# A hybrid trunk layer in fp32: the retention state term as three rounded matmuls, masks loaded per head, three instead of four transposes for a head's last keys, and the last output rows in four pieces

## The chip, the cores and the metric

The kernel runs on one core of a Trainium2 chip. The metric is device time in microseconds (us) of one launch; lower is better. The engines are named as the profile names them: PE (matmul), PEld (weight loads of PE), DVE (vector), ACT (scalar), POOL (GpSimd) and SP (which here issues most of the DMAs). Each engine runs its own instructions in a fixed order and waits on semaphores for the others.

## The reference, cut to what matters

One layer over 1024 positions of width 1024, all in fp32: an RMS norm, one wide input projection, a retention branch and a recurrent branch side by side, a gated merge, an output projection, then a gated MLP and a last RMS norm. Nearly all of the arithmetic is in the large projections. The change touches the retention branch, which has four heads with keys of 128 and values of 256:

```python
    def step(state, inp):
        qi, ki, vi = inp
        scores = jnp.einsum("bhid,bhjd->bhij", qi, ki) * intra_decay
        out = (jnp.einsum("bhij,bhjv->bhiv", scores, vi)
               + jnp.einsum("bhid,bhdv->bhiv", qi * q_decay[:, :, None], state))
        state = (state * chunk_decay[:, None, None]
                 + jnp.einsum("bhjd,bhjv->bhdv", ki * k_decay[:, :, None], vi))
        return state, out
...
    y_a = (o * jax.nn.silu(g_ret.astype(jnp.float32))).astype(x.dtype) @ w_ret_o[l]
...
    return rms_norm(x, norm_f_w)
```

## The kernel before, in words

**Large products.** Every large projection is a set of 128x512 matmuls on operands that were split beforehand into a rounded high part and a rounded rest (`split`: an ACT copy that rounds, line 597, and a DVE subtraction, line 598). A product takes three such rounded passes, high by high, high by low and low by high (`PASSES`). The large matmuls are issued at line 848 (`mm_fast`), those of the values at 1606; the blocks of weights (`w` tiles) are split up to seven ahead of their use. Sums of blocks (lines 683 to 692, 871, 877) save one product in eight.

**Side work.** While PE works through a list of jobs, generators in the queue `back` are advanced a little after each product. Among them are the retention heads (`retention_head`, after `rotary_head`), the recurrent blocks (`lru_block`, matmuls at 1257), and sums of weights that are put away for later (`four_sums`, 1429 to 1441). A head works through its 1024 positions in eight blocks of 128, numbered `h` (half) and `b`. For each block PE makes the scores (1372), DVE masks them (1375), the result is split (597 and 598 on `sm` tiles), PE multiplies them by the values in three rounded passes (1380), and adds the term of the carried state: one matmul of the unrounded query block and the unrounded state `rst` (1382), 28 times in all, since a head's first block has no state. Then ACT copies the output (1387), PE makes the state's increment from keys and values in three passes (1392), DVE adds it to the decayed state (1396, or 1394 for the first), and DVE takes the statistics of the output (1400, 1401). The state has two buffers, `rst[0]` and `rst[1]`, which change places. `keys` turns a half's keys by four transposes (1332), scales them (1337) and splits them; the last block of a head makes no increment, yet its keys are transposed too.

**Constants.** The tile `cst` holds small columns, four 128x128 masks, one per head, and the identity. It is loaded in one DMA (1695); before that its first columns serve as a place for the first columns of `x` (1630 to 1635).

**The end.** The last rows leave in `final_half`: when the last product of 128x256 is done, ACT squares it (2059), DVE adds (2060), POOL takes the power (2066), and ACT and DVE each scale a 128x512 tile (2076, 2074), which then leaves by one DMA each (2077), after the two tiles of `final` (2087, 2090).

**Order.** The kernel is written in program order, and then a planner (`Plan`) reads its instructions with their dependencies, and writes an order for each engine by its own table of durations. It tries 150 drafts with random shifts and keeps one; the program is then built again with this order as a chain on each engine. A small edit therefore changes the order of unrelated instructions as well.

Of the kernel before, what the change touches and what calls it, by code (L numbers as in the profile page):

```python
# [38 lines left out]

C_INVF, C_KDEC, C_GEPS, C_MASK, C_ID = 0, 1, 5, 9, 9 + 512  # L40
NCONST = 9 + 512 + 128
# [512 lines left out]
def tile_trunk_layer(ctx, tc, x, xt, front, positions, params, consts, normf, w_in, w_v, w_ro, w_lo,  # L554
# [10 lines left out]
    U = Units(pool, "u", NU, [P, TH], now)  # L565
    sm = Units(pool, "sm", 6, [P, P], now)
    psg = Units(pps, "g", 6, [P, TH], now)
# [4 lines left out]
    par = pool.tile([P, NPAR], F32, tag="par", name="par")  # L572
    cst = pool.tile([P, NCONST], F32, tag="cst", name="cst")
    ident = cst[:, C_ID:C_ID + P]
# [487 lines left out]
    rcol = pool.tile([P, 8], F32, tag="rcol", name="rcol")  # L1062
    row = pool.tile([8, P], F32, tag="row", name="row")
    kdr = pool.tile([P, HEADS, 8], F32, tag="kdr", name="kdr")

    def x_rms():
# [20 lines left out]
        PE.transpose(j[0:8, 0:P], rcol, ident)  # L1087
        S.copy(row, j[0:8, 0:P])
        psa.put(j)
        SY.dma_start(r_d.rearrange("h (t p) -> (h t) p", p=P), row)  # L1090
        for h in range(2):
# [211 lines left out]
    qk, gg = {}, {}  # L1303
    rst = [pool.tile([P, 256], F32, tag=f"state{i}", name=f"state{i}") for i in range(2)]
    bst = pool.tile([P, 4, 6], F32, tag="bst", name="bst")
# [22 lines left out]
    def keys(hd, qk, h):  # L1328
        ps = psa.get()
        for b in range(4):  # L1330
            bs = slice(128 * b, 128 * b + 128)
            PE.transpose(ps[:, bs], qk[1, h][:, bs], ident)
        t = get()
        for b in range(4):
            bs = slice(128 * b, 128 * b + 128)
            n = 4 * h + b
            S.activation(t[:, bs], ps[:, bs], AF.Copy, scale=kdr[:, hd, n:n + 1])
        kd[h] = split(t)
        put(t, late=SOONER)
        psa.put(ps)  # L1340

    def v_tile(hd, h, g):
        t = get()
        SY.dma_start(t, v_d[hd, 2 * h + g].rearrange("p b c -> p (b c)"))
        return t

    def retention_head(hd, qk):
        cur = 0
        tick = now[0]
        raw = {(0, g): v_tile(hd, 0, g) for g in range(2)}  # L1350
        yield from landed(tick)

# [5 lines left out]
        v_split(0, 0)  # L1358
        mask = cst[:, C_MASK + 128 * hd:C_MASK + 128 * hd + 128]
        for h in range(2):  # L1360
            for b in range(4):
# [11 lines left out]
                s = sm.get()  # L1373
                n = 4 * h + b
                V.scalar_tensor_tensor(s, p1[:, 0:128], rcol[:, n:n + 1], mask, ALU.mult, ALU.mult)
                psa.put(p1)
# [4 lines left out]
                if not first:  # L1381
                    PE.matmul(p2[:, 0:256], qk[0, h][:, bs], rst[cur], start=False, stop=True)  # L1382
                sm.put(*s)
# [5 lines left out]
                if not last:  # L1389
                    p3 = psa.get()  # L1390
                    for n, (i, j) in enumerate(PASSES):
                        PE.matmul(p3[:, 0:256], kd[h][i][:, bs], v[j][:, vs], start=n == 0, stop=n == 2)  # L1392
                    if first:
                        V.tensor_copy(rst[1 - cur], p3[:, 0:256])
                    else:
                        V.scalar_tensor_tensor(rst[1 - cur], rst[cur], GAM128[hd], p3[:, 0:256],
                                               ALU.mult, ALU.add)
                    psa.put(p3)
                    cur = 1 - cur
                V.bn_stats(bst[:, b, :], o)  # L1400
# [161 lines left out]
    def values():  # L1562
# [23 lines left out]
        def x_set(nm, j, first=False):  # L1586
            hi, lo = get(F32R), get(F32R)
            b, w = xs[nm, j], cst[:, j:j + 1] if nm == "B11" else wn(nm, j)
            if not first:
                S.activation(hi, b, AF.Copy, scale=w)  # L1590
            for c in (slice(0, P), slice(P, TH)) if first else (slice(0, TH),):
                if first:
                    V.tensor_scalar(hi[:, c], b[:, c], w, None, ALU.mult)
                V.scalar_tensor_tensor(lo[:, c], b[:, c], w, hi.bitcast(F32)[:, c], ALU.mult, ALU.subtract)
            h1[nm, j] = (hi, lo)
# [35 lines left out]
        nc.scalar.dma_start(cst[:, 0:first], front[:, 0:first])  # L1631
        xs["B11", 0] = cst[:, 8:8 + TH]
        V.tensor_copy(par[:, 0:8], cst[:, 0:8])
        wload("A11", 0)
        SY.dma_start(cst[:, first:8 + TH], front[:, first:])
        wload("A11", 1)
# [36 lines left out]
        for j in range(4):  # L1673
            f[j], t[j], s[j] = get(), get(), vget()
            S.activation(f[j], xs["B11", j], AF.Copy, scale=wn("B11", j))
            if j:
                put(xs["B11", j])
            V.tensor_add(s[j], raw["A21", j], raw["A22", j])
# [14 lines left out]
        for j in range(4):  # L1693
            xload("B22", j)
        SY.dma_start(cst, consts)
        back.append(x_rms())
# [356 lines left out]
    def final_half(u, s):  # L2053
# [16 lines left out]
        put(j)  # L2070
        for c in range(2):
            t = fin.pop((0, 0)) if c == 0 else o
            if c:
                V.tensor_scalar(t, t, r, None, ALU.mult)
            else:
                S.activation(t, t, AF.Copy, scale=r)
            (SY if c else nc.scalar).dma_start(out[128 * 3:128 * 4, TH * c:TH * c + TH], t)
            put(t)

# [111 lines left out]
```

## Time and profile before

| What | Value |
|---|---|
| median of 3 runs | 1567.7 us (1567.51 to 1568.17) |
| the profiled execution's own time | 1566.78 us |
| its span, first to last instruction | 1565.0 us |
| PE busy | 1557.1 us, 99% of the span |
| DVE busy | 1343.9 us, 86% |
| ACT busy | 952.5 us, 61% |
| granted PE clock | 0.999 |
| moved by DMA | 278.97 MB, mean 178 GB/s |

The shares are means over stages: retention lies between about 230 and 433 us of the span, the merge and output projections between 640 and 890, the MLP behind that. Since PE is busy nearly always, what counts is where PE waits, what the other engines have to deliver to it in a stage, and what lies before its first and behind its last matmul. The profiled execution took 0.9 us less than the median of the runs.

### The profile page before, as it was taken

The numbers are of one execution on the slowest core, as the hardware profiler recorded it, in microseconds if no ns is written. First come the engines' busy times: TensorE is split into PE (matmuls) and PEld (weight loads), VectorE is DVE, ScalarE is ACT, GpSimd is POOL, SyncE is SP. The second block draws the span as 40 slices with busy tenths as digits, with TensorE's granted clock in tenths as the row PEclk, the third lists the DMA queues.
The fourth block names the chain that finished last, engine by engine and source line by source line (L and its number), as shares of the span: only waits on it lengthen the run. The fifth ranks groups of instructions, "written<-read, shape, count | busy, mean of one in ns | idle before, by whom it ended". The sixth has DMA issues, their size and how long they took to land.

```text
span 1565.0 us, 21570 instructions
## 1 busy us (share of the span) xinstructions
PE 1557.1 (99%) x7057; PEld 1290.7 (82%) x7057; DVE 1343.9 (86%) x2397; ACT 952.5 (61%) x1675; POOL 61.0 (4%) x81
## 2 busy tenths in 40 slices
PE   9999999999999999999999999999999999999998
PEld 7888888888888888888888888888888888888887
DVE  8999988998899988999998899777777778887875
ACT  8558766766568777855456665455454547554653
POOL 0001000000000000000000001000000000000000
PEclk9999999999999999999999999999999999999999
DMA  9344334454364346875995336444444476777752
GB/s 328 121 139 130 115 129 124 140 187 155 114 203 142 101 135 186 266 276 174 315 315 173 106 115 223 141 135 142 134 138 144 146 239 196 250 266 256 265 187 80
DMA packets 157713, 278.97 MB, mean 178 GB/s; under 512 B 17048, under 2 KB 29728, under 8 KB 157600
## 3 DMA queue, kind: packets, MB, share of 16 engines
q1 hardware_dynamic: 152080, 261.79, 51.3%
q0 software_dynamic: 4224, 13.64, 2.7%
q10 hardware_dynamic: 1296, 2.17, 0.4%
q8 instruction: 55, 0.90, 0.2%
q14 instruction: 58, 0.48, 0.1%
HBM read 192.59 MB, written 83.89 MB: 177 GB/s over the span
## 4 chain that ended last, share of the span: by engine, by line
PE 93%; DMA 3%; DVE 2%; ACT 1%; issue 1%; SPq 0%; POOLq 0%; POOL 0%; DVEq 0%; ACTq 0%
PE g L848 81%; PE g L1606 5%; PE a L1257 3%; DMA w<-mix_d 1%; PE a L1382 1%; PE a L1380 1%; DMA u<-tw_d 1%; PE a L1392 1%; DVE w L598 0%; PE a L1884 0%; PE a L1372 0%; PE a L1451 0%; DMA w<-w_lo 0%; DMA sg_d<-u 0%; DVE u L598 0%
## 5 line engine op out<-in xcount | busy, mean ns | idle before, releaser
L848 PE MATMUL g<-u,w 128*128 128x512 f32 x6060 | 1412.6, 391 | 0.0
L848 PEld LDWEIGHTS g<-u,w 128*128 128x128 f32 x6060 | 1129.7, 188 | 229.0
L597 ACT CAST w<-w 128x512 fp32r<-128x512 f32 x519 | 319.0, 621 | 334.4 <-PE g L848 240.3
L598 DVE TENSOR_TENSOR w<-w,w 128x512 fp32r<-128x512 f32 x519 | 352.9, 684 | 84.4 <-ACT w L597 81.0
L597 ACT CAST u<-u 128x512 fp32r<-128x512 f32 x253 | 151.2, 619 | 60.6 <-DVE u L1239 7.5
L598 DVE TENSOR_TENSOR u<-u,u 128x512 fp32r<-128x512 f32 x253 | 166.7, 682 | 4.3 <-ACT u L597 4.0
L900 ACT COPY u<-g 128x512 f32<-128x512 f32 x148 | 86.4, 583 | 61.3 <-PE g L848 58.4
L877 DVE TENSOR_TENSOR u<-g,u 128x512 f32<-128x512 f32 x146 | 100.1, 686 | 22.1 <-PE g L848 16.8
L1936 DVE SCALAR_TENSOR_TENSOR u<-u,par,u 128x511 f32<-128x511 f32 (+1 forms) x96 | 71.6, 746 | 12.8 <-ACT u L1933 12.2
L1606 PE MATMUL g<-w,u 128*128 128x512 f32 x252 | 58.7, 389 | 0.0
L1606 PEld LDWEIGHTS g<-w,u 128*128 128x128 f32 x252 | 47.2, 188 | 9.9
L1941 POOL DMA_DIRECT2D ff_d<-u x48 | 36.2, 754 | 444.6 <-DVE u L1940 434.2
L683 DVE TENSOR_TENSOR w<-w,w 128x512 f32<-128x512 f32 x72 | 49.2, 683 | 2.7 <-DMA w<-ff_d 1.4
L897 ACT COPY g<-g 128x512 f32<-128x512 f32 x70 | 40.4, 577 | 17.8 <-PE g L848 17.6
L1257 PE MATMUL a<-u,u 128*128 128x512 f32 x192 | 50.4, 390 | 0.5 <-ACT u L597 0.5
L686 DVE TENSOR_TENSOR w<-w,w 128x512 f32<-128x512 f32 x72 | 49.3, 684 | 0.7
L689 DVE TENSOR_TENSOR w<-w,w 128x512 f32<-128x512 f32 x72 | 49.2, 683 | 0.3 <-DMA w<-w_lo 0.2
L692 DVE TENSOR_TENSOR w<-w,w 128x512 f32<-128x512 f32 x72 | 49.2, 683 | 0.4
L1933 ACT ACTIVATE u<-u,par 128x512 f32<-128x512 f32 x48 | 39.1, 816 | 7.8 <-DVE u L877 7.0
L1257 PEld LDWEIGHTS a<-u,u 128*128 128x128 f32 x192 | 35.9, 188 | 8.6 <-ACT u L597 1.3
L871 DVE TENSOR_TENSOR u<-u,u 128x512 f32<-128x512 f32 x34 | 23.2, 687 | 20.5 <-ACT u L900 20.4
L1940 DVE TENSOR_TENSOR u<-u,u 128x512 f32<-128x512 f32 x48 | 32.9, 687 | 5.4 <-ACT u L1939 5.4
(216 smaller groups left out, 1158.8 us busy)
## 6 DMA issues: line engine op xcount, KB each, us to landing
w<-w_in SPq DMA_DIRECT2D x96, 256.0 KB, 2.8
w<-w_up SPq DMA_DIRECT2D x96, 256.0 KB, 2.7
u<-w_dn SPq DMA_DIRECT2D x84, 256.0 KB, 3.2
u<-x_d SPq DMA_DIRECT2D x52, 256.0 KB, 4.4
x_d<-u SPq DMA_DIRECT2D x48, 256.0 KB, 3.6
ff_d<-u POOLq DMA_DIRECT2D x48, 256.0 KB, 2.9
td_d<-u SPq DMA_DIRECT2D x48, 256.0 KB, 3.0
u<-td_d SPq DMA_DIRECT2D x48, 256.0 KB, 4.5
```

The lines of the kernel that those rows point to most:

```text
L597: S.copy(hi, src)
L598: V.tensor_sub(lo, src, hi.bitcast(F32))
L683: V.tensor_add(s, r["A21"], r["A22"])
L686: V.tensor_sub(s, s, r["A11"])
L689: V.tensor_sub(s, r["A12"], s)
L692: V.tensor_sub(src, r["A21"], r["A11"])
L848: PE.matmul(bank[:, s], w[a][:, c], need(op, (SETS[nm], j))[b][:, s], start=first and n == 0, stop=n == 11, skip_group_check=True)
L877: V.tensor_add(u, bank, u)
L900: S.copy(u, bank)
L1257: PE.matmul(ps, wg[g][a][:, cs], xs[k][b], start=q == 0, stop=q == 5)
L1606: PE.matmul(bank, o[p][:, c], w[q], start=first and j == n == 0, stop=j == 3 and n == 2, skip_group_check=True)
L1936: V.scalar_tensor_tensor(c[:, s:], src[:, :TH - s], w, c[:, s:], ALU.mult, ALU.add)
```

## The change

- The state term becomes three rounded passes. The query block is split (an ACT copy and a DVE subtraction of 128x128 into two more `sm` tiles, of which there are now 8 instead of 6); the new state is split after each of its updates into `rsp[0]` and `rsp[1]` (an ACT copy and a DVE subtraction of 128x256). The unrounded state has one buffer now and is updated in place.
- `keys` makes three transposes and three scalings instead of four for a head's second half, and splits 384 columns instead of 512.
- `cst` keeps the small columns and the identity; a tile `mask` of 128x128 is loaded by one SP DMA at the start of each head. The row of inverse norms lies in an `sm` tile.
- The first block of `x` gets a `u` tile of its own, and is loaded in full (512 instead of 384 columns), while its first 128 columns are still taken from `cst`.
- The last two tiles are scaled and sent in halves of 256 columns, two for ACT and two for DVE and SP.

```diff
-C_INVF, C_KDEC, C_GEPS, C_MASK, C_ID = 0, 1, 5, 9, 9 + 512
+C_INVF, C_KDEC, C_GEPS, C_ID, C_MASK = 0, 1, 5, 9, 9 + 128
...
-    sm = Units(pool, "sm", 6, [P, P], now)
+    sm = Units(pool, "sm", 8, [P, P], now)
...
     def keys(hd, qk, h):
-        ps = psa.get()
-        for b in range(4):
+        ps, count = psa.get(), 4 - h
+        for b in range(count):
...
-        kd[h] = split(t)
+        kd[h] = get(F32R), get(F32R)
+        c = slice(0, 128 * count)
+        S.copy(kd[h][0][:, c], t[:, c])
+        V.tensor_sub(kd[h][1][:, c], t[:, c], kd[h][0].bitcast(F32)[:, c])
...
+        SY.dma_start(mask, consts[:, C_MASK + 128 * hd:C_MASK + 128 * hd + 128])
         yield from landed(tick)
...
-        mask = cst[:, C_MASK + 128 * hd:C_MASK + 128 * hd + 128]
...
+                if not first:
+                    q = split(qk[0, h][:, bs], sm.get)
                 V.scalar_tensor_tensor(s, p1[:, 0:128], rcol[:, n:n + 1], mask, ALU.mult, ALU.mult)
...
                 if not first:
-                    PE.matmul(p2[:, 0:256], qk[0, h][:, bs], rst[cur], start=False, stop=True)
+                    for n, (i, j) in enumerate(PASSES):
+                        PE.matmul(p2[:, 0:256], q[i], rsp[j], start=False, stop=n == 2)
+                    sm.put(*q)
...
                     if first:
-                        V.tensor_copy(rst[1 - cur], p3[:, 0:256])
+                        V.tensor_copy(rst, p3[:, 0:256])
                     else:
-                        V.scalar_tensor_tensor(rst[1 - cur], rst[cur], GAM128[hd], p3[:, 0:256],
-                                               ALU.mult, ALU.add)
+                        V.scalar_tensor_tensor(rst, rst, GAM128[hd], p3[:, 0:256], ALU.mult, ALU.add)
                     psa.put(p3)
-                    cur = 1 - cur
+                    S.copy(rsp[0], rst)
+                    V.tensor_sub(rsp[1], rst, rsp[0].bitcast(F32))
...
-        xs["B11", 0] = cst[:, 8:8 + TH]
+        xs["B11", 0] = get()
         V.tensor_copy(par[:, 0:8], cst[:, 0:8])
         wload("A11", 0)
-        SY.dma_start(cst[:, first:8 + TH], front[:, first:])
+        SY.dma_start(xs["B11", 0], front[:, 8:8 + TH])
...
-        SY.dma_start(cst, consts)
+        SY.dma_start(cst, consts[:, 0:C_MASK])
...
-        for c in range(2):
-            t = fin.pop((0, 0)) if c == 0 else o
-            if c:
-                V.tensor_scalar(t, t, r, None, ALU.mult)
-            else:
-                S.activation(t, t, AF.Copy, scale=r)
-            (SY if c else nc.scalar).dma_start(out[128 * 3:128 * 4, TH * c:TH * c + TH], t)
-            put(t)
+        t = fin.pop((0, 0)), o
+        for s in (slice(0, TH // 2), slice(TH // 2, TH)):
+            for c in range(2):
+                if c:
+                    V.tensor_scalar(t[c][:, s], t[c][:, s], r, None, ALU.mult)
+                else:
+                    S.activation(t[c][:, s], t[c][:, s], AF.Copy, scale=r)
+                (SY if c else nc.scalar).dma_start(out[128 * 3:128 * 4, TH * c + s.start:TH * c + s.stop], t[c][:, s])
+        put(*t)
```

What the planner makes of it shows at three places. In the rows below, `a` is a PSUM bank for small products, `g` one for large products, `u`, `w` and `sm` are tiles, and a `u` or `w` pair with neighbouring numbers is the high and the low part of a split. The first place is PE in the second block of the first head. Before:

```order
L1380 MATMUL a_63_2569<-u_438_2532,sm_14_2565 128x256
L1380 MATMUL a_63_2569<-u_439_2533,sm_14_2565 128x256
L1392 MATMUL a_65_2575<-u_438_2532,u_433_2482 128x256
L1380 MATMUL a_63_2569<-u_438_2532,sm_15_2566 128x256
L1382 MATMUL a_63_2569<-state_87,u_417_2241 128x256
L848 MATMUL g_76_2284<-u_106_265,w_415_2237 128x512
```

And now (line numbers of the changed kernel: 1387 was 1380, 1390 was 1382, 849 was 848):

```order
L1387 MATMUL a_63_2579<-u_440_2536,sm_20_2575 128x256
L1387 MATMUL a_63_2579<-u_441_2537,sm_20_2575 128x256
L1387 MATMUL a_63_2579<-u_440_2536,sm_21_2576 128x256
L849 MATMUL g_76_2287<-u_106_266,w_415_2240 128x512
L849 MATMUL g_76_2287<-u_108_274,w_415_2240 128x512
L1390 MATMUL a_63_2579<-parts_87,sm_18_2570 128x256
L849 MATMUL g_76_2287<-u_109_275,w_415_2240 128x512
L1390 MATMUL a_63_2579<-parts_88,sm_18_2570 128x256
L1390 MATMUL a_63_2579<-parts_87,sm_19_2571 128x256
```

The one matmul that read the state and the query became three that read the state's parts and the query's, and large matmuls stand between them here. The second place is DVE at the same block, from the masking of its scores to that of the next block's. Before:

```order
L1375 SCALAR_TENSOR_TENSOR sm_13_2563<-a_61_2561,rcol,cst 128x128
L1394 COPY state_87<-a_59_2550 128x256
L598 TENSOR_TENSOR sm_15_2566<-sm_13_2563,sm_14_2565 128x128
L598 TENSOR_TENSOR u_443_2558<-u_436_2487,u_442_2557 128x512
L598 TENSOR_TENSOR w_450_2365<-w_444_2339,w_449_2364 128x512
L1396 SCALAR_TENSOR_TENSOR state_86<-state_87,a_65_2575 128x256
L598 TENSOR_TENSOR u_450_2607<-u_447_2582,u_449_2606 128x512
L1400 BN_STATS bst<-u_441_2548 128x6
L1401 BN_AGGR mv<-bst 128x2 x2
```

And now (1382 was 1375, 599 was 598, 1403, 1405 and 1409 were 1394, 1396 and 1400; 1408 is new):

```order
L1382 SCALAR_TENSOR_TENSOR sm_17_2569<-a_61_2567,rcol,mask 128x128
L1403 COPY state<-a_59_2554 128x256
L599 TENSOR_TENSOR sm_21_2576<-sm_17_2569,sm_20_2575 128x128
L599 TENSOR_TENSOR u_445_2564<-u_438_2490,u_444_2563 128x512
L1408 TENSOR_TENSOR parts_88<-state,parts_87 128x256
L1409 BN_STATS bst<-u_443_2552 128x6
L1405 SCALAR_TENSOR_TENSOR state<-state,a_65_2587 128x256
L599 TENSOR_TENSOR sm_39_2636<-u_419_2244,sm_38_2635 128x128
L599 TENSOR_TENSOR w_450_2368<-w_444_2342,w_449_2367 128x512
L599 TENSOR_TENSOR u_452_2629<-u_449_2596,u_451_2628 128x512
L1408 TENSOR_TENSOR parts_88<-state,parts_87 128x256
```

Between two maskings DVE has two more kinds of subtraction, that of the state (1408) and that of a query block two blocks ahead (599 on `sm_39`). The third place is ACT at the end of the program. Before:

```order
L2059 ACTIVATE u_3032_15570,nst<-g_466_15541 128x256
L2059 ACTIVATE u_3032_15570,nst<-g_467_15555 128x256
L2090 DMA out<-u_3019_15531 128x512
L2076 ACTIVATE u_3008_15511<-u_3008_15511,nst 128x512
L2077 DMA out<-u_3008_15511 128x512
```

And now (2068 was 2059, 2100 was 2090, 2086 and 2087 were 2076 and 2077):

```order
L2068 ACTIVATE u_3034_15793,nst<-g_466_15764 128x256
L2068 ACTIVATE u_3034_15793,nst<-g_467_15778 128x256
L2100 DMA out<-u_3021_15754 128x512
L2086 ACTIVATE u_3010_15734<-u_3010_15734,nst 128x256 x2
L2087 DMA out<-u_3010_15734 128x256 x2
```

ACT scales both halves first and issues both DMAs behind them; SP likewise has two DMAs of 128x256 behind its last one of 128x512.

More of the change, by code (lines that the diff above doesn't have):

```diff
@@ L572, in tile_trunk_layer @@
     par = pool.tile([P, NPAR], F32, tag="par", name="par")
-    cst = pool.tile([P, NCONST], F32, tag="cst", name="cst")
+    cst = pool.tile([P, C_MASK], F32, tag="cst", name="cst")
+    mask = pool.tile([P, P], F32, tag="mask", name="mask")
     ident = cst[:, C_ID:C_ID + P]
@@ L1062, in tile_trunk_layer @@
     rcol = pool.tile([P, 8], F32, tag="rcol", name="rcol")
-    row = pool.tile([8, P], F32, tag="row", name="row")
     kdr = pool.tile([P, HEADS, 8], F32, tag="kdr", name="kdr")
@@ L1087, in x_rms @@
         PE.transpose(j[0:8, 0:P], rcol, ident)
-        S.copy(row, j[0:8, 0:P])
+        row = sm.get()
+        S.copy(row[0:8, :], j[0:8, 0:P])
         psa.put(j)
-        SY.dma_start(r_d.rearrange("h (t p) -> (h t) p", p=P), row)
+        SY.dma_start(r_d.rearrange("h (t p) -> (h t) p", p=P), row[0:8, :])
+        sm.put(row)
         for h in range(2):
@@ L1303, in tile_trunk_layer @@
     qk, gg = {}, {}
-    rst = [pool.tile([P, 256], F32, tag=f"state{i}", name=f"state{i}") for i in range(2)]
+    rst = pool.tile([P, 256], F32, tag="state", name="state")
+    rsp = [pool.tile([P, 256], F32R, tag=f"parts{i}", name=f"parts{i}") for i in range(2)]
     bst = pool.tile([P, 4, 6], F32, tag="bst", name="bst")
@@ L1333, in keys @@
         t = get()
-        for b in range(4):
+        for b in range(count):
             bs = slice(128 * b, 128 * b + 128)
@@ L1347, in retention_head @@
     def retention_head(hd, qk):
-        cur = 0
         tick = now[0]
         raw = {(0, g): v_tile(hd, 0, g) for g in range(2)}
+        SY.dma_start(mask, consts[:, C_MASK + 128 * hd:C_MASK + 128 * hd + 128])
         yield from landed(tick)
@@ L1591, in x_set @@
             for c in (slice(0, P), slice(P, TH)) if first else (slice(0, TH),):
+                bc = cst[:, 8:8 + P] if first and c.start == 0 else b[:, c]
                 if first:
-                    V.tensor_scalar(hi[:, c], b[:, c], w, None, ALU.mult)
-                V.scalar_tensor_tensor(lo[:, c], b[:, c], w, hi.bitcast(F32)[:, c], ALU.mult, ALU.subtract)
+                    V.tensor_scalar(hi[:, c], bc, w, None, ALU.mult)
+                V.scalar_tensor_tensor(lo[:, c], bc, w, hi.bitcast(F32)[:, c], ALU.mult, ALU.subtract)
             h1[nm, j] = (hi, lo)
@@ L1675, in values @@
             S.activation(f[j], xs["B11", j], AF.Copy, scale=wn("B11", j))
-            if j:
-                put(xs["B11", j])
+            put(xs["B11", j])
             V.tensor_add(s[j], raw["A21", j], raw["A22", j])
```

## The prediction

> **What bounds the kernel now.** I read the page first. PE is busy 99% of the span, and the chain of work that ended last lies on PE for 93%:
>
> ```profile
> PE 1557.1 (99%) x7057; PEld 1290.7 (82%) x7057; DVE 1343.9 (86%) x2397; ACT 952.5 (61%) x1675; POOL 61.0 (4%) x81
> DVE  8999988998899988999998899777777778887875
> PE 93%; DMA 3%; DVE 2%; ACT 1%; issue 1%; SPq 0%; POOLq 0%; POOL 0%; DVEq 0%; ACTq 0%
> ```
>
> In the second row, DVE's busy tenths in slices of 39 us, DVE is nearly full up to 900 us, and only then has room. A busy PE could still be waiting between matmuls, since their ends are modelled. So I looked at the chain in order of time (start, length, what) for long stretches without a break, and at PE's waits:
>
> ```profile
> 81.64 55.99 PE g L848 x247
> 637.31 116.52 PE g L848 x514
> 890.37 665.59 PE g L848 x2936
> PE g L1641 <- DVE st L1816: 1.0, 1, 1.0
> PE a L1257 <- ACT u L597: 0.5, 1, 0.5
> PE a L1884 <- DVE u L1878: 0.2, 1, 0.2
> ```
>
> 55.99/247, 116.52/514 and 665.59/2936 are all 0.2267 us: a large matmul costs that wherever it stands, in 666 us without a gap. The waits come to 1.7 us, 1.0 of them before the first matmul. To see what is left beside those, I priced PE's whole list, by line and shape (count, then busy time and mean; the mean of one overlaps its successor, so I take spacings instead):
>
> ```profile
> L848 PE MATMUL g<-u,w 128*128 128x512 f32 x6036 | 1409.8, 391 | 0.0
> L1606 PE MATMUL g<-w,u 128*128 128x512 f32 x252 | 58.7, 389 | 0.0
> L1257 PE MATMUL a<-u,u 128*128 128x512 f32 x192 | 50.4, 390 | 0.5 <-ACT u L597 0.5
> L1382 PE MATMUL a<-state,u 128*128 128x256 f32 x56 | 16.6, 378 | 0.0
> ```
>
> The three big groups, and 84 more matmuls of 128x512 in the opening, are 6564 x 0.2267 = 1488 us. The small ones come to about 64 us (by the spacings below), together 1552 us of the 1557.1 that the page calls busy. So some 5 us in all are lost to waits and joints, and the other 8 us of the span lie before and behind PE's work. A change can gain by taking work off PE, by those 5 us, or at the two ends; anything else is under PE's cover. It loses where it makes PE wait.
>
> **PE's own work in the state term.** The unrounded matmul of the state shows as two rows each (x56 for 28). Its price is read from starts in the timeline of PE (start, length of the merged piece):
>
> ```profile
> 247.62 0.52 PE L1380 MATMUL a<-u,sm 128*128 128x256 f32 x3
> 247.98 0.59 PE L1382 MATMUL a<-state,u 128*128 128x256 f32 x2
> 248.22 1.96 PE L848 MATMUL g<-u,w 128*128 128x512 f32 x7
> 250.03 0.60 PE L1332 MATMUL a<-cst,u 128*128 128x128 f32 x4
> 250.38 2.54 PE L848 MATMUL g<-u,w 128*128 128x512 f32 x10
> 252.75 0.52 PE L1380 MATMUL a<-u,sm 128*128 128x256 f32 x3
> 253.11 0.60 PE L1382 MATMUL a<-state,u 128*128 128x256 f32 x2
> 253.35 0.58 PE L848 MATMUL g<-u,w 128*128 128x512 f32 x1
> 253.78 0.40 PE L1392 MATMUL a<-u,u 128*128 128x256 f32 x2
> ```
>
> Three rounded passes of 128x256 take 252.75 to 253.11, 0.36 us, and 247.62 to 247.98 the same. For the state one must not stop at the next start: from 253.11 to 253.35 it seems to take 0.24 us, but the large matmul recorded at 253.35 is then followed only at 253.78. Both together take 0.67 us, and 0.67 - 0.2267 = 0.44. The earlier place gives 250.03 - 247.98 - 7 x 0.2267 = 0.46. So a state term goes from 0.44 to 0.46 us down to 0.36: 28 x (0.08 to 0.10) = 2.2 to 2.8 us off PE; I take 2.3, from the lower end, since the passes are now often apart from each other, between large matmuls, and each joint costs something.
>
> The reading decides the sign. Taken at its face, 0.24 us, the state term would rise by 28 x 0.12 = 3.4 us; I drop it because it leaves a large matmul of 0.43 us, which no stretch without a state term has. The Trainium skill (FP8 and Floating Point Precision, TensorE Precision Notes) says that a true FP32 matmul is four passes through the array. The trace agrees in kind, since 0.44 is nearer to four rounded passes than to the two that are shown; by the rule, with 0.12 us a pass, it would be 0.48 us, and the term 28 x 0.12 = 3.4 us instead of 2.3, off PE.
>
> Four transposes from 250.03, with the ten large matmuls behind them, end at 252.75: 2.72 - 2.267 = 0.45 us, 0.11 each. The change drops one per head: 4 x 0.11 = 0.4 us. PE's work falls by 2.7 us (2.2 to 3.2 by the ends above).
>
> **What DVE and ACT get on top.** All of it falls into the retention stage. Its windows (length; busy time and count of PE, PEld, DVE, ACT, POOL), one stage ahead of it for comparison, then DVE's and ACT's nearest rows, and the first and the last of twelve rows of DVE's waits there, 19.8 us together:
>
> ```profile
> 80.00:196.00 116.00, 115.51 (x510) 95.34 (x509) 112.97 (x229) 83.21 (x124) 4.32 (x8) 1.00 0.40 127
> 230.00:433.00 203.00, 202.94 (x1052) 171.81 (x1052) 181.60 (x395) 129.06 (x274) 8.21 (x7) 1.00 0.45 144
> L598 DVE TENSOR_TENSOR sm<-sm,sm 128x128 fp32r<-128x128 f32 x32 | 9.1, 285 | 1.4 <-ACT sm L597 1.3
> L1396 DVE SCALAR_TENSOR_TENSOR state<-state,a 128x256 f32<-128x256 f32 x24 | 9.9, 414 | 2.1 <-PE a L1392 2.0
> L597 ACT CAST sm<-sm 128x128 fp32r<-128x128 f32 x32 | 9.5, 296 | 9.9 <-DVE sm L1375 9.7
> L1387 ACT COPY u<-a 128x256 f32<-128x256 f32 x32 | 11.9, 372 | 26.9 <-PE a L1382 22.9 <-DVE rs L1411 2.8 <-PE a L1380 1.0
> DVE bst L1400 <- ACT u L1387: 5.0, 10, 0.8
> DVE u L877 <- PE g L848: 0.3, 1, 0.3
> ```
>
> Twenty-eight query splits and 28 state splits cost DVE at most 28 x (0.285 + 0.414) = 19.6 us; back to back, instructions overlap by about 0.08 us (two subtractions of 0.68 each take 1.29 together at 9.36 in the timeline of the opening, the row is shown further down), so at least 28 x (0.205 + 0.334) = 15 us. The shorter split of the last keys gives back 0.5 (four times 128 columns of 512, at (0.68 - 0.285)/3 = 0.13 us). I take 15 us. DVE is idle there for 203 - 181.6 = 21.4 us, so it fits, but leaves 6 us: 97% busy. That is the load of the stage from 80 to 196 (112.97 of 116), which PE went through with 115.51 us busy, so 97% alone does not stall PE: weights are split up to seven blocks of 12 matmuls ahead, 7 x 12 x 0.2267 = 19 us. If that cover went, each microsecond of DVE would be one of PE. ACT gets 28 x (0.296 + 0.372) = 18.7 us and by the new order five more table loads (52 for 47; one of 1.28 us stands in the opening); with 203 - 129 = 74 us idle it has room.
>
> **The added wait.** The state's parts have one buffer each. ACT's rounding of the new state waits for the three matmuls on the old one, DVE's subtraction waits for ACT, and PE's next state term waits for both; behind them on DVE stand statistics and weight splits. This adds about 0.37 + 0.41 = 0.8 us and two hand-overs to a path that goes round once per block. A block takes the time between two scores, four to eight us in the new order by PE's work (starts of the state terms in the rows above: 247.98 and 253.11, 5.1 us). So it is hidden, unless DVE's queue stands still in front of it. I put down 0.5 us for new waits of PE in the 28 blocks: zero is one end, and the other that the whole 0.8 us shows in one block in eight at each head's start and its middle, 8 x 0.8 = 6 us.
>
> **Masks and constants.** Four DMAs of 64 KB more on SP, one of 324 KB shrinks to 68 KB: as many bytes as before. A mask's DMA waits on SP for the last masking of the head before, and a weight load stands behind it. In the new order it stands among the loads of `four_sums` and the stores of the head before, long after that masking. Zero; at worst one weight load is late by an SP issue, 0.4 us, under the 19 us of blocks ahead.
>
> **Both ends.** At the start (rows of the opening's timeline), the first block's later columns now come with 64 KB more, and DVE subtracts the first weights before it rounds these columns:
>
> ```profile
> 4.55 0.41 DVE L1593 TENSOR_SCALAR u<-cst 128x384 fp32r<-128x384 f32 x1
> 4.88 0.68 DVE L598 TENSOR_TENSOR w<-w,w 128x512 fp32r<-128x512 f32 x1
> 6.70 0.72 ACT L1590 ACTIVATE u<-u,cst 128x512 fp32r<-128x512 f32 x1 [0.79 <-DMA u<-xt]
> 9.36 1.29 DVE L598 TENSOR_TENSOR w<-w,w 128x512 fp32r<-128x512 f32 x2
> 1.18 1.28 ACT L1638 ACT_TABLE_LOAD   x1 [1.18 <-PEq L2176]
> ```
>
> The columns lose 0.6 us, the weights' rests win 0.3, and the order of the twelve first matmuls follows. ACT's rounding at 6.70 waited for a load, which 64 KB ahead of it delay by 0.2 us. Between 0.2 us won and 0.2 lost, I take zero. At the end:
>
> ```profile
> 1559.60 0.69 POOL L2066 TENSOR_TENSOR nst<-nst,half 128x1 f32<-128x1 f32 x1 [1.23 <-DVE nst L2060]
> 1560.28 0.33 SPq L2090 DMA_DIRECT2D out<-u  x1
> 1560.32 0.72 ACT L2076 ACTIVATE u<-u,nst 128x512 f32<-128x512 f32 x1 [0.99 <-POOL nst L2066]
> 1560.84 0.33 SPq L2077 DMA_DIRECT2D out<-u  x1
> 1561.07 0.34 ACTq L2077 DMA_DIRECT2D out<-u  x1
> ```
>
> Three DMAs of 256 KB are issued from 1560.28 to 1561.41, and the span ends at 1565.0. In halves, ACT's first scaling is done 0.2 to 0.3 us earlier (an estimate: half of 0.72 would be 0.36, less a fixed part), but its two activations pay that part twice, and both queues have one issue of 0.33 us more, so the last bytes are issued 0.2 us later and the first 0.2 us earlier. The bytes are the same. Zero, between 0.3 us won and 0.5 lost.
>
> **The sum.** -2.7 on PE, +0.5 for waits, 0 for masks and both ends: -2.2 us. From the profiled execution's 1566.78 us that is 1564.6; from the median, 0.9 us above it, 1567.7 - 2.2 = 1565.5 us. A measurement of this kernel tells a change from none at about 0.2%, 3.1 us: faster is below 1564.6, slower above 1570.8.
>
> **The rivals.**
> 1. *The new order also clears old waits.* The 5 us beside PE's work are up for a new draw; a gain of another 1 to 2 us gives 1563.5 to 1564.5. For it: the planner weighs all waits anew. Against: most of these us are small joints, not waits.
> 2. *An unrounded pass costs as much as a rounded one.* Then the state term goes from 4 x 0.12 to 0.36: 3.4 us, and 1567.7 - 3.4 - 0.4 + 0.5 = 1564.4. The rows above (0.44 and 0.46) speak against it. This is what the Trainium skill's four passes of FP8 and Floating Point Precision, TensorE Precision Notes, would give.
> 3. *The gain is given back.* The state's longer path shows as 0.1 us in each of the 28 blocks, 2.8 us: 1567.7 us, no change. For it: DVE's own waits in the stage (5.0 us for ACT's output copies alone) show that its queue does stand still.
> 4. *DVE becomes the bound of the retention stage.* DVE's idle time there is nearly all waits for PE and ACT, 19.8 of 21.4 us. If all of these stay, 15 - 1.6 = 13.4 us do not fit, and PE stands still for what the weight blocks split ahead do not cover: nothing of it if they are full (19 us), 7.1 us if they are a third full. The latter gives 1567.7 - 2.7 + 7.1 = 1572.1. It decides from 5.8 us of DVE work that find neither room nor cover (2.7 + 3.1). Against: sums for later (`four_sums`) can move behind the stage, and 80 to 196 us ran at this load.
>
> **Chances.** The forecast (gain of 1 to 3.1 us) 0.52; rivals 1 and 2 0.20 and 0.05, both faster; rival 3 (from 1 us gained to 3.1 lost) 0.14, same; rival 4 0.09, slower. Faster 0.25, same 0.66, slower 0.09. The range goes down to 3.2 us off PE with 1.2 us of old waits gone, 1563.3, and up to a gain given back with 1.2 us on top, 1568.9; rival 4 and half of the far end of rival 1 lie outside.
>
> **What would show it.** PE's rows of the state term should be 84 with 0.12 us between starts where they stand together, 28 transposes of keys instead of 32, and the chain from 890 us to the end unchanged but earlier by 2 us. In the window of the retention stage DVE should be at 195 us or more of 201. I am wrong if PE's waits name the state's parts or weight splits for more than 2 us in that stage, if the stretch behind 433 us has new gaps, or if the span behind the last matmul grows by over 0.5 us.

## The result: 2.5 us faster, about as much as PE's own list lost

Over 16 runs of each the changed kernel takes 1565.3 us (median; 1563.59 to 1566.96) and the kernel before 1567.81 (1566.48 to 1569.67). The ratio is 0.9985, with a 95% interval of 0.9978 to 0.9992: a gain that can be told from none, and smaller than the 0.2% that the prediction took for the least that counts. The forecast was 1565.5.

The page of the changed kernel, the rows that answer to those of before:

```profile
span 1563.0 us, 21782 instructions
PE 1555.2 (99%) x7081; PEld 1289.0 (82%) x7081; DVE 1356.7 (87%) x2454; ACT 971.2 (62%) x1733; POOL 64.5 (4%) x81
DVE  8999989999999988999998898777777778887885
PE 96%; ACT 2%; DMA 1%; issue 0%; DVE 0%; POOLq 0%; POOL 0%; SPq 0%; ACTq 0%
```

PE has 24 matmul records more (28 x 3 for 28 x 2, and four transposes less) and is busy 1.9 us less. DVE has 12.8 us more to do. The state's parts in the view by line and shape (busy time, mean ns of one, idle time before):

```profile
L1390 PE MATMUL a<-parts,sm 128*128 128x256 f32 x84 | 14.9, 279 | 0.0
L1335 PE MATMUL a<-cst,u 128*128 128x128 f32 x28 | 4.4, 272 | 0.0
```

The new state term in the timeline of PE (start, length):

```profile
251.84 0.52 PE L1390 MATMUL a<-parts,sm 128*128 128x256 f32 x3
252.19 0.40 PE L849 MATMUL g<-u,w 128*128 128x512 f32 x1
252.43 0.39 PE L1401 MATMUL a<-u,u 128*128 128x256 f32 x2
```

The three passes take 252.19 - 251.84 = 0.35 us, and the large matmul behind them 0.24: no half of it is hidden there, as it was behind the unrounded matmul. All that the view of waits shows of PE in the whole program (total, times, longest), then the retention stage's window (length, then the busy time of PE, PEld, DVE, ACT and POOL, the granted clock and DMA), then DVE's two largest waits in that stage:

```profile
PE g L1651 <- DVE st L1825: 1.0, 1, 1.0
PE g L849 <- ACT u L901: 0.5, 2, 0.3
```

```profile
230.00:433.00 203.00, 203.00 (x1088) 172.98 (x1088) 194.52 (x456) 143.37 (x329) 12.28 (x8) 1.00 0.46 147
```

```profile
DVE u L1323 <- ACT u L1320: 1.2, 2, 0.6
DVE rs L1420 <- POOL rs L1419: 0.9, 1, 0.9
```

DVE is busy 194.52 us of the 203, 12.9 more than before, and PE is never idle there. DVE's own waits in the stage fell from 19.8 us to 7.2 (the sum of 13 rows, the two largest shown): the new work went where DVE had stood waiting.

To compare kernels I price every matmul of a profile by its kind's spacing (0.2267 us for 128x512, 0.119 for a rounded 128x256, 0.43 for the unrounded state, 0.213 for the scores, 0.108 for a transpose) and take the rest of the time up to the last matmul's start as time beside the list: waits, joints, the slower matmuls of the opening. The 0.43 is what a fit over all its places gives (0.42 to 0.43 in the eight profiles that have this matmul). Each row is one profiled execution; the ratio is that of the timed runs.

| Kernel | Ratio to before, 95% | Span | PE's list | Beside it | Last matmul to end |
|---|---|---|---|---|---|
| before | 1 | 1565.0 | 1551.9 | 6.6 | 6.5 |
| changed | 0.9985 (0.9978 to 0.9992) | 1563.0 | 1549.4 | 7.2 | 6.3 |
| state unrounded again | 0.9998 (0.9990 to 1.0007) | 1566.2 | 1551.5 | 8.4 | 6.3 |
| keys only | 1.0003 (0.9994 to 1.0012) | 1565.9 | 1551.5 | 8.0 | 6.5 |
| tail only | 1.0000 (0.9991 to 1.0009) | 1565.7 | 1551.9 | 7.2 | 6.7 |
| places only | 1.0008 (0.9999 to 1.0017) | 1566.9 | 1551.9 | 8.8 | 6.2 |
| before, second seed | 1.0009 (1.0001 to 1.0018) | 1568.5 | 1551.9 | 10.1 | 6.5 |
| changed, second seed | 1.0016 (1.0008 to 1.0025) | 1568.7 | 1549.4 | 12.9 | 6.3 |
| before, third seed | 0.9993 (0.9984 to 1.0002) | 1565.0 | 1551.9 | 6.7 | 6.5 |
| changed, third seed | 0.9983 (0.9975 to 0.9992) | 1565.0 | 1549.4 | 9.2 | 6.3 |
| subtractions twice | 0.9992 (0.9983 to 1.0001) | 1564.4 | 1549.4 | 8.7 | 6.3 |
| changed, 300 drafts | 0.9982 (0.9973 to 0.9991) | 1564.5 | 1549.4 | 8.8 | 6.3 |

From before to changed: the list -2.5, beside it +0.6, the end -0.1, in sum -2.0 us of span. A profiled execution is one draw and not the median: that of the kernel before took 1.0 us less than the median of its 16 runs, that of the changed kernel 0.5 us less, that of before with the second seed 1.9 us more. Taken to the medians, before and changed lose about equally much beside the list (some 7.7 us both), and the 2.5 us between the timed runs are about what the list lost. Differences of a microsecond in the fifth column can be chance of the execution.

### The profile page after: what moved, and what is told of

The parts are those of the page before. It is cut to its first block, busy times and chain, and to the rows that moved or that the text cites. A ratio compares the mean times of both kernels' runs of the same rounds, so it can differ in the third digit from the quotient of the medians.

```text
span 1563.0 us, 21782 instructions
## 1 busy us (share of the span) xinstructions
PE 1555.2 (99%) x7081; PEld 1289.0 (82%) x7081; DVE 1356.7 (87%) x2454; ACT 971.2 (62%) x1733; POOL 64.5 (4%) x81
## 4 chain that ended last, share of the span: by engine, by line
PE 96%; ACT 2%; DMA 1%; issue 0%; DVE 0%; POOLq 0%; POOL 0%; SPq 0%; ACTq 0%
PE g L849 85%; PE g L1616 5%; PE a L1259 3%; PE a L1387 1%; DMA u<-td_d 1%; PE a L1401 1%; PE a L1390 1%; PE a L1893 0%; PE a L1377 0%; PE a L1460 0%; ACT w L598 0%; ACT u L598 0%; PE a L1335 0%; DMA cst<-front 0%; ACT L1215 0%
## 5 line engine op out<-in xcount | busy, mean ns | idle before, releaser
L598 ACT CAST u<-u 128x512 fp32r<-128x512 f32 x245 | 146.7, 619 | 59.1 <-PE g L849 7.5
L599 DVE TENSOR_TENSOR u<-u,u 128x512 fp32r<-128x512 f32 x245 | 161.9, 686 | 6.3 <-ACT u L598 2.4
L901 ACT COPY u<-g 128x512 f32<-128x512 f32 x148 | 86.2, 582 | 60.3 <-PE g L849 57.4
L1945 DVE SCALAR_TENSOR_TENSOR u<-u,par,u 128x511 f32<-128x511 f32 (+1 forms) x96 | 71.7, 748 | 12.8 <-ACT u L1942 12.2
L872 DVE TENSOR_TENSOR u<-u,u 128x512 f32<-128x512 f32 x34 | 23.2, 688 | 20.5 <-ACT u L901 20.4
L1206 ACT COPY u<-g 128x512 f32<-128x512 f32 x56 | 32.5, 581 | 8.8 <-PE g L849 8.8
```

What stands on the lines that cost most here:

```text
L598: S.copy(hi, src)
L599: V.tensor_sub(lo, src, hi.bitcast(F32))
L901: S.copy(u, bank)
L1945: V.scalar_tensor_tensor(c[:, s:], src[:, :TH - s], w, c[:, s:], ALU.mult, ALU.add)
```

## The experiments

**The parts alone.** First the changed kernel with the state term of before; keys, places and tail stay changed.

```diff
-                    for n, (i, j) in enumerate(PASSES):
-                        PE.matmul(p2[:, 0:256], q[i], rsp[j], start=False, stop=n == 2)
-                    sm.put(*q)
+                    PE.matmul(p2[:, 0:256], qk[0, h][:, bs], rst[cur], start=False, stop=True)
...
-                    S.copy(rsp[0], rst)
-                    V.tensor_sub(rsp[1], rst, rsp[0].bitcast(F32))
+                    cur = 1 - cur
```

> The changed kernel with the state term put back to one unrounded matmul (two state buffers, no splits of state and query); keys, places of the constants and the tail stay changed. Theory (the time is PE's list plus waits, and the state term went from 0.45 to 0.36 us): PE's list is 2.1 to 2.8 us longer than in the changed kernel and only 0.4 shorter than before; time 0.4 us below before, 1567.4 against 1567.8. Rival (the gain came from the new order, the places or the tail): it keeps the gain, 1565.3. Rival (the state term's longer path cost something): below 1565.

Measured 1567.73 us beside 1567.64 for the kernel before on that chip: the gain is gone, as the theory has it. But the profile does not let it stand as a clean proof. The list is 2.1 us longer than in the changed kernel, and 1.2 us lie elsewhere: the first 20 us lost 3.2 us to the opening instead of 0.9, so the rest of the program lost 1.1 us less than in the changed kernel. The list is the part that a new order cannot move; what lies beside it was drawn anew here too.

Then the other three parts, each alone on the kernel before: the keys, the tail, and the places (masks, constants, first block of `x`, small tiles).

```diff
-        for b in range(4):
+        for b in range(count):
...
-        xs["B11", 0] = cst[:, 8:8 + TH]
+        xs["B11", 0] = get()
...
+        for s in (slice(0, TH // 2), slice(TH // 2, TH)):
```

> The kernel before with only the three instead of four transposes, scalings and the shorter split for a head's last keys. Theory: 4 x 0.11 = 0.4 us less on PE's list, time 0.4 us below before give or take 1 us for a new order's waits. Rival (the dropped ACT and DVE work frees the retention stage): 1 us or more less in waits as well.

> The kernel before with only the last rows in four pieces. Theory: nothing, the stretch from the last matmul's start to the end of the span stays within 0.2 us of 6.46; PE's list is the same, and time within 1 us of before by the new order. Rival (the tail is bound by the last issue): 0.3 to 0.5 us shorter. Rival (more issues and smaller packets): up to 0.5 us longer.

> The kernel before with only the places changed: a mask per head by its own DMA, small constants, the row in a small tile, the first block of x in its own tile, 8 small tiles. Theory: PE's list is the same to 0.1 us, the first 20 us lose between 0.2 us less and 0.2 us more than before, time within 1 us of before. Rival (the mask's DMA holds up the SP queue): PE waits for weights in the retention stage, 1 us or more.

None of the three gives a gain that can be measured. The keys take their 0.4 us off the list, and the new order loses 1.3 beside it; the rival's freed waits did not come. The tail brings the end of the program nothing: in its one profile the end is 0.2 us longer. The places kept the list, and lost 2.2 us beside it, 1.7 of them between 640 and 890 us (2.6 us there against 0.9 before), long after the masks were loaded. Their time, 1.2 us above before, lies just outside what I had allowed, and their first 20 us lost 0.4 us more instead of 0.2 at most. In the retention stage, where the rival would have it, they lost 3.5 us against 2.9. Of PE's waits in the whole program only the last row below lies in that stage, and it is not for weights (two waits of 0.2 us for weights are in the opening):

```profile
PE a L1886 <- DVE u L1880: 1.4, 1, 1.4
PE g L1644 <- DVE st L1818: 1.0, 1, 1.0
PE a L1382 <- ACT u L1339: 0.3, 2, 0.2
```

**The price of the state term.** The same term twice, once in each kernel, prices both forms. Nothing else is edited, but the order is drawn anew.

```diff
-                    PE.matmul(p2[:, 0:256], qk[0, h][:, bs], rst[cur], start=False, stop=True)
+                    for twice in range(2):
+                        PE.matmul(p2[:, 0:256], qk[0, h][:, bs], rst[cur], start=False, stop=twice == 1)
```

> The kernel before with the unrounded state matmul issued twice into the same bank, 28 more (the state term is counted twice). It prices that matmul by itself. Theory: 0.44 to 0.46 us each as read behind the following large matmul, 12.3 to 12.9 us more than before, 1580.0 to 1580.6. Rival (the price is the distance to the next recorded start, 0.24): 6.7 us more. Rival (four passes at the price of a rounded one, 0.48): 13.4 us more. Waits of a new order are good for 1 us either way, so the spacings in the profile have to separate the last two.

Measured 1580.16 us beside 1567.41: 12.75 us for 28 matmuls, 0.455 each. That is the theory's value, and nearly twice the 0.24 us of the next recorded start, which would have given 6.7 us. The interval of the ratio, 11.1 to 15.4 us, takes in the 13.4 of four rounded passes too, so these two only the spacing can tell apart. In PE's timeline of this kernel, four records of the state term are followed by five large matmuls:

```profile
237.99 1.03 PE L1383 MATMUL a<-state,u 128*128 128x256 f32 x4
238.66 1.50 PE L848 MATMUL g<-u,w 128*128 128x512 f32 x5
240.01 0.38 PE L1372 MATMUL a<-u,u 128*128 128x128 f32 x2
```

240.01 - 237.99 - 5 x 0.2267 = 0.89 us for two, 0.44 each. From 237.99 to 238.66, the next recorded start, it would be 0.67, which is not even twice 0.24: only the last record of a run shows too short. The run's time has 0.01 us more per matmul than this spacing, and redrawn waits: its profile loses 1.3 us more beside the list than that of before. The same with the rounded passes, in the changed kernel:

```diff
-                    for n, (i, j) in enumerate(PASSES):
-                        PE.matmul(p2[:, 0:256], q[i], rsp[j], start=False, stop=n == 2)
+                    for n, (i, j) in enumerate(PASSES * 2):
+                        PE.matmul(p2[:, 0:256], q[i], rsp[j], start=False, stop=n == 5)
```

> The changed kernel with the three rounded passes of the state term issued twice, 84 more matmuls of 128x256 (the state term is counted twice). Theory: 0.12 us each, 10.0 us more than the changed kernel, 1575.4. Rival (a joint between a small and a large matmul costs as well, and the passes stand apart): 11 us or more.

Measured 1575.4 us: 10.1 more than the changed kernel's 1565.3 (measured on another chip, where the kernel before took 1567.81; here it took 1567.41), 0.12 each; by the ratios it is 10.5 us, 0.125 each, with 2 us of uncertainty, so the time alone does not exclude the rival's 11. In its timeline six in a row take 243.14 - 242.43 = 0.71 us, 0.118 each:

```profile
242.43 0.87 PE L1390 MATMUL a<-parts,sm 128*128 128x256 f32 x6
243.14 1.32 PE L849 MATMUL g<-u,w 128*128 128x512 f32 x5
```

So a state term went from 0.43 to 0.455 us, by spacing and by time, to 0.36, 28 times: 2.0 to 2.7 us. Four passes of the rounded price, the sum by the Trainium skill's rule (FP8 and Floating Point Precision, TensorE Precision Notes), would have been 13.4 us for the first of these two kernels, 0.48 each; the spacing gives 0.43 to 0.44, so the rule is right in kind and about a tenth high as a price.

**The order.** The planner's shifts were drawn with another seed, in both kernels.

```diff
-        r = np.random.RandomState(1)
+        r = np.random.RandomState(2)
```

> The kernel before with another seed for the planner's random shifts: the same instructions in another order. Theory: PE's list is the same; waits beside it, 5.7 us before, are drawn anew, between 4.7 and 6.7 us; time within 1 us of before. Rival (the order matters more than the change): 2 us or more away from before.

> The changed kernel with that same other seed. Theory: PE's list as in the changed kernel, 2.5 us below that of before; time 1.5 to 3.5 us below before. Rival (the gain was a lucky order): less than 1 us below before.

The kernel before took 1568.56, 1.15 us above 1567.41, just outside the 1 us that I had allowed; its profile lost 3.5 us more beside the list, not 1 (it took 1.9 us more than the median). The changed one took 1569.98, the slowest order of all, and missed what I expected by 4 us. Its retention stage is as good as with the first seed (3.0 us beside the list, 2.7 there). The loss stands at one place, in PE's waits, in POOL's timeline, and in the windows around it (of PE alone: length, busy time, then granted clock and DMA):

```profile
PE a L1087 <- POOL rcol L1085: 3.0, 1, 3.0
```

```profile
66.70 6.90 POOL L1085 TENSOR_TENSOR rcol<-nst,half 128x8 f32<-128x8 f32 x1 [66.25 <-DVE nst L1084]
```

```profile
66.00:70.00 4.00, 4.00 (x19) 1.00 0.19 38
70.00:73.36 3.36, 0.62 (x3) 1.00 0.62 213
73.36:76.77 3.41, 3.12 (x8) 0.50 0.33 107
76.77:80.00 3.23, 3.23 (x15) 1.00 0.96 264
```

The power that makes the inverse norms took POOL 6.90 us. It took 1.65 in the profile of the changed kernel, and 1.65 to 2.62 in the other twelve. PE came to the transpose of its result 3.9 us after the power's start (the matmul ahead ends at 70.62), stood still for 3.0 us, and then worked at half the granted clock, in a window of 3.41 us in which eight matmuls took the time of fifteen. Together that cost 4.7 us between 20 and 230 us, where the first seed's order lost none. Nothing of the change touches that power, and the first order leaves it no more room: there too PE's transpose stands 3.7 us behind its start (66.4 and 70.1).

What the power waited for shows beside it on DVE. First DVE with the second seed, then DVE and POOL in the changed kernel with the first:

```profile
66.53 0.74 DVE L1754 SCALAR_TENSOR_TENSOR u<-u,par,u 128x512 f32<-128x512 f32 x1
67.20 1.28 DVE L599 TENSOR_TENSOR w<-w,w 128x512 fp32r<-128x512 f32 x2
68.40 1.88 DVE L599 TENSOR_TENSOR u<-u,u 128x512 fp32r<-128x512 f32 x3
70.21 1.28 DVE L599 TENSOR_TENSOR w<-w,w 128x512 fp32r<-128x512 f32 x2
71.41 0.68 DVE L599 TENSOR_TENSOR u<-u,u 128x512 fp32r<-128x512 f32 x1
72.01 0.68 DVE L1749 TENSOR_TENSOR u<-g,u 128x512 f32<-128x512 f32 x1
```

```profile
66.25 0.69 DVE L1749 TENSOR_TENSOR u<-g,u 128x512 f32<-128x512 f32 x1
66.42 1.65 POOL L1085 TENSOR_TENSOR rcol<-nst,half 128x8 f32<-128x8 f32 x1 [65.98 <-DVE nst L1084]
```

In all five profiles with 1.65 us DVE was, when the power began, in a sum that reads a PSUM bank (`u<-g,u`), as in the second fence. In the other nine it was in an instruction whose inputs are all tiles of the other on-chip memory, SBUF (`u`, `w`, `par`), and the power ended 0.98 or 1.6 us after the start of DVE's next sum from a bank or next `u<-u,par,u`. With the second seed eight subtractions of splits stand in a row, and that next one starts only at 72.01; the power ends at 73.60. The smaller power of the retention heads (`rs`, 128x4) shows the same in these profiles: about 1.0 us nearly everywhere where DVE is idle or reads a bank when it begins, 1.2 to 3.2 where DVE is in an instruction on SBUF tiles. So the loss lies in the order that DVE got here, and not in one execution: the mean granted clock, 0.999 or 1.0 in every run of the other kernels, is 0.997 or 0.998 in nine of the eleven of this one. No run moved those subtractions alone, so this is read from the traces and not tried. A third seed was to tell a single slow power from a property of the change; by these clocks it was neither, but a property of that order:

> The kernel before with a third seed for the planner. Theory: PE's list as before, waits between 6.5 and 10 us counted from the start of the span (seven orders of nearly the same work so far gave 6.7 to 10.1), time from before to 2.5 us above.

> The changed kernel with that third seed. With the second seed it lost 4.7 us to one POOL power of 6.9 us (1.65 to 2.6 in the other profiles) and the half clock behind the stop. Theory (that was one slow power, not a property of the change): PE's list 2.5 us below that of before, waits 7 to 10 us, and time 1 to 3 us below that of the kernel before with the same seed. Rival (the change makes good orders rarer): level with it or slower.

On this chip the kernel before took 1568.44 us; with the third seed it took 1566.78, and the changed one 1566.01. Its power took 2.02 us. The changed kernel is 0.8 us faster than its partner in time and 0.0010 in ratio, less than the 1 to 3 us of the theory. The two intervals overlap, but seven of its eleven runs are faster than its partner's fastest, so it is not level as the rival has it. Three seeds give -0.0015, +0.0007 and -0.0010 between the partners, in the mean -0.0006 or 0.9 us, less than half of what the list lost; beside the list the changed kernel lost more than its partner in all three profiles. Three draws are too few to say that the change makes good orders rarer, and too few to exclude it.

**DVE's room.** Both new subtractions of every block twice:

```diff
                     q = split(qk[0, h][:, bs], sm.get)
+                    V.tensor_sub(q[1], qk[0, h][:, bs], q[0].bitcast(F32))
...
-                    V.tensor_sub(rsp[1], rst, rsp[0].bitcast(F32))
+                    for twice in range(2):
+                        V.tensor_sub(rsp[1], rst, rsp[0].bitcast(F32))
```

> The changed kernel with DVE's two new subtractions of every block issued twice: 28 x (0.205 + 0.334) = 15 us more DVE work in the retention stage, nothing new for PE. DVE was busy 194.5 of 203 us there, so 8.5 us were free. Theory (blocks split ahead and sums that move out of the stage cover the rest): PE's waits in the stage rise by less than 2 us, time 1565 to 1567.5. Rival (DVE is the bound of the stage from here on): 6.5 us or more do not fit and show, 1571.8 or more.

Measured 1566.3 us, ratio 0.9992: within 1.1 us of the changed kernel by the ratios, and not slower than before. The windows behind the retention stage of the changed kernel, whose retention stage stands above, and then all three of this one (DVE's busy time stands behind that of PE and PEld):

```profile
433.00:470.00 37.00, 37.00 (x169) 30.58 (x168) 33.82 (x60) 26.82 (x44) 0.00 (x0) 1.00 0.55 183
470.00:640.00 170.00, 169.91 (x750) 140.29 (x749) 154.26 (x263) 135.44 (x207) 0.00 (x0) 1.00 0.48 156
```

```profile
230.00:433.00 203.00, 202.91 (x1079) 172.38 (x1078) 197.87 (x486) 140.86 (x321) 8.58 (x7) 1.00 0.43 140
433.00:470.00 37.00, 36.86 (x171) 29.78 (x170) 36.89 (x74) 24.24 (x41) 1.01 (x1) 1.00 0.59 205
470.00:640.00 170.00, 169.90 (x748) 139.95 (x747) 158.63 (x272) 146.22 (x220) 0.00 (x0) 1.00 0.48 156
```

DVE took 3.4 us more in the stage, 3.1 more up to 470 us and 4.4 more from there to 640, 10.8 in sum and not 15: other work moved behind the stage. No wait of PE stands in the view between 230 and 640 us, but where DVE is full, 36.89 of 37 us, PE's time beside the list rose from 0.1 to 1.0 us. The rival's 6.5 us are excluded, but the 0.9 us can be a sign that DVE's room ends here.

**A better order.**

```diff
-    DRAFTS, REACH, THROW = 150, 4e4, 1000.0
+    DRAFTS, REACH, THROW = 300, 4e4, 1000.0
```

> The changed kernel with 300 instead of 150 drafts for the planner, the first 150 being those of the changed kernel: a try at a version that beats both. Theory (most of what is left beside PE's list is joints and chance of an execution): within 1 us of the changed kernel, 1564.3 to 1566.3. Rival (waits are what the drafts remove): 1 to 3 us below it.

Ratio 0.9982 against the changed kernel's 0.9985: the same within the intervals. Twice as many drafts find nothing that the chip shows; 8.8 us lie beside its list, more than the 7.2 of the kernel that it started from.

## Why the prediction was right, step by step

- **PE's work, -2.7 us.** The list fell by 2.5: 2.1 for the state term at 0.43 us and 0.4 for the transposes. Reading the unrounded matmul past the next recorded start decided the sign; issued twice, it cost 0.455 us, and the rounded three 0.36. The face value of 0.24 us is refuted, and the 0.48 of rival 2 by the spacing alone.
- **New waits, +0.5 us.** They came to 0.6 beside the list in the two profiles, and to about nothing by the medians. They are not where I put them: in the retention stage the time beside the list fell, from 2.9 to 2.7 us, and no wait of PE stands there, so the state's longer path costs PE nothing that shows. This hangs on the price: at 0.455 us a state term before has 2.2 us there, and the changed kernel 0.5 more. The new order lost 1.0 us behind 890 us, where before had 0.1, at two places where PE waits for an ACT copy of a large product (0.5 us in PE's waits, the rest around them), won 0.8 between 20 and 230, and lost 0.1 to 0.3 in each of the opening and the two stages from 433 to 890. New gaps behind 433 us were one of the signs of being wrong that I had named, and here they are:

```profile
1399.98 76.45 PE L849 MATMUL g<-u,w 128*128 128x512 f32 x336 [0.24 <-ACT u L901]
1476.72 80.23 PE L849 MATMUL g<-u,w 128*128 128x512 f32 x364 [0.29 <-ACT u L901]
```

That the size came near was chance: I had priced a mechanism, and what these profiles show is a draw of the order.
- **DVE's 15 us on top.** 12.9 by the windows, 97% foreseen and 96% measured; the rival that DVE becomes the bound (rival 4) fell twice, by this and by the subtractions issued twice. Its assumption that DVE's waits stay failed: they went from 19.8 to 7.2 us.
- **Masks and constants, zero; both ends, zero.** In the first 20 us the changed kernel lost 0.9 us beside the list, before 0.7. At the end:

```profile
1557.73 0.68 POOL L2075 TENSOR_TENSOR nst<-nst,half 128x1 f32<-128x1 f32 x1 [1.23 <-DVE nst L2069]
1558.83 0.88 SPq L2087 DMA_DIRECT2D out<-u  x2
1558.99 0.84 ACTq L2087 DMA_DIRECT2D out<-u  x2
```

From POOL's power to the end of the span it is 1563.0 - 1557.73 = 5.27 us, and was 1565.0 - 1559.60 = 5.40. The last issues start later behind the power than before, as forecast; the end gains 0.1 us all the same. The six other profiles with the four pieces and the changed places have 6.33 to 6.35 us from the last matmul to the end, as the changed kernel has; the tail alone has 6.7. Those without the pieces have 6.45 to 6.47, and the places alone 6.2.
- **Rival 1, old waits cleared,** did not come: of fourteen profiles only that of the third seed on the kernel before matches the 6.6 us beside the list with which this comparison began, in an execution 1.0 us below the median. Rival 3, the gain given back, is what happened with the second seed, by another mechanism than the one I named.

What stays open: whether the row of subtractions on DVE is what held POOL's power for 6.90 us, since no run moved it alone. Open too is how much of the 2.5 us another draw would keep: that the list is shorter is sure, the time beside it differs by some 2 us from order to order, without the one long power, and the mean of three draws is a gain of 0.9 us.

## What to carry to other kernels

Where PE is busy 99% of the span, price its list first, by spacings over runs of matmuls that end in several ordinary ones; a single next start can be wrong by a factor of two and turn the sign. Work on another engine can be nearly free as long as its own waits, not only its idle time at the end, can take it: here DVE took 12.9 us more in a stage that seemed 89% full, and 3.4 more after that, with 7.5 moved behind the stage. When a planner redraws the whole order for each edit, an effect below its spread needs several draws on both sides, and the list of the bounding engine is the part that can be read from one profile. An engine that is nearly idle can still stop the others: look at what runs beside its longest instruction.

## What the runs showed of the hardware

- Behind a stop of PE of 3.0 us its granted clock was 0.50 for 3.41 us (73.36 to 76.77 in the windows above), so the stop cost 4.7 us. The Trainium skill (TensorE: Matmul & The Clock Gate, Part 1) says that the clock falls to half after an idle window of about 3.4 us and rises after a busy one; the trace agrees on the length of the slow stretch, and shows it after a stop somewhat shorter than that window: the clock falls 2.7 us after the last matmul's recorded end (70.62).
- The opening was slower by more than the wait in a profile that waited longer for its first weights. With the state unrounded again, PE waited 0.9 us for the first weights; the twelve first matmuls then took 4.9 us, 0.41 each, and the next ones began at 10.39. In the changed kernel the ten that follow its own short wait take 2.5 us, 0.25 each, and the next begin at 7.72. That the wait is the cause is not shown; it is one execution of each. First the former, then the latter, from PE's timeline:

```profile
5.45 5.10 PE L1664 MATMUL g<-w,u 128*128 128x512 f32 x12 [0.86 <-ACT w L598]
10.39 3.83 PE L1612 MATMUL g<-w,u 128*128 128x512 f32 x16
```

```profile
5.20 2.68 PE L1668 MATMUL g<-w,u 128*128 128x512 f32 x10
7.72 6.51 PE L1616 MATMUL g<-w,u 128*128 128x512 f32 x28
```

- A power of 128x8 on POOL took 1.65, 2.0 to 2.1, 2.6 or 6.9 us in different kernels, the same operation on tiles of the same shape. Its time went with what DVE ran beside it, in all fourteen profiles: 1.65 us beside a sum that reads a PSUM bank, more beside instructions on SBUF tiles alone, and 6.9 us beside eight subtractions in a row.
